# A decoder layer on one core: the first norm's shift and scale by halves, queries and keys in one 512-wide projection, and the MLP operands of the last 512 tokens in two steps

## The chip, the cores and the metric

One core of a Trainium2 chip runs the whole kernel in one launch. The metric is the time of that launch in device microseconds. The engines are TensorE (PE in the profile, its weight loads PEld), VectorE (DVE), ScalarE (ACT), GpSimd (POOL) and SyncE (SP), which issues most of the transfers. Each engine works through its own list of instructions in order; semaphores make one engine wait for another.

## What is computed

The reference is one layer of a decoder: 1024 tokens of width 1024, in float32.

```
h  = rmsnorm(x, g_mix) * (1 + scale_a) + shift_a      # scale, shift, gate: columns of act(c) @ ada_w + ada_b
qkv = h @ w_in                                         # 2960 columns, four groups of 4 heads x 64
o  = [differential, forgetting, stick-breaking, sparse attention] per head group
x1 = x + gate_a * (o @ w_out)
h2 = rmsnorm(x1, g_ffn) * (1 + scale_m) + shift_m
u  = h2 @ w_up ; gate, val = split(u)                  # 2 x 2816 columns
out = x1 + gate_m * ((silu(conv3(gate)) * val) @ w_down)
```

The six vectors (shift, scale and gate for the two sub-layers) are each a product of one vector of 1024 with a 1024 x 1024 block of `ada_w`, 4 MB each.

## The kernel before

The program first writes down all its operations in program order (`K.mm`, `K.act`, `K.dma` and so on), with the tiles that they read and write. Each tile has a class with a quota of buffers. `K.schedule` then plans: it gives every operation a time from a table of costs, and on each engine takes the one that is earliest in program order among those that are ready. What comes out is a fixed list for each engine; on the chip nothing is reordered. Line 393 is the place where every operation is recorded, so all instructions have that line in the profile, and tiles tell them apart.

Every product of two float32 matrices is made from three matmuls: each operand is split into a high part (a cast to the format of fp32r) and a low part (operand minus high part), and high x high, low x high and high x low are added in one PSUM bank.

The start of the program goes like this. `load_x(0)` loads four tiles of 128 tokens (`x`) and scales their rows by the root mean square. `ada_part(1)` and then `ada_part(0)` form the scale and the shift: for each of 8 blocks of 128 rows of `ada_w` (1024 columns, tile `ada`) VectorE does one multiply-add into `acc`, and TensorE then sums the 128 partitions by matmuls against ones (`Xa<-ones,acc`, one column for each of the 8 blocks of 128 features). `norm_x` (line 701) transposes x on TensorE (`X`) and calls `modulate` (line 738): ScalarE applies scale and shift while it moves the bank to `hx`, VectorE casts the high part of `hT`, VectorE or GpSimd subtracts for the low part. The index k counts the 8 blocks of 128 features, and a product with `w_in` adds up all 8.

`proj` (line 765) loads a piece of `w_in`, splits it (the cast on ScalarE, the subtraction on GpSimd) and multiplies it with the tokens, one bank for each tile of 128 tokens (j, 8 of them). Before the change there are four such projections ahead of the attention: queries of group A (`p_aq`, 256 columns), values of group A (`p_va`, 256), values and small columns of C, D and B (`vcd`, 400) and keys of group A (256). Beside them, `ada_rest` forms the other four vectors, in 64 blocks of 512 columns (`ada2`); `merge` mixes its operations into the program, 9.0 planned microseconds apart. Attention follows, group A, C, D and B (`S` are scores, `T` transposes, `O` outputs), with later projections (`pP`) mixed in.

After attention comes the output projection (`op`), and for each half of 512 tokens the second norm: four tiles `xn` are transposed (`oy`), ScalarE applies shift and scale, and the MLP's operands are formed. The MLP uses seven products of quarter blocks in place of eight, so it needs sums and differences of the two token halves: for each of 4 blocks, four subtractions (`hf`, `hk`) and five operands `gB`, each split into a cast and a subtraction. `up` are the banks of the first MLP product, `fr` raw weights, `fw` split ones. Products 1 and 2 (`mul_first`) need the first token half only (`gA`); the five others need `gB`, in the order 6, 5, 7, 3, 4.

Of the kernel before, what the change touches and what calls it, by code (L numbers as in the profile page):

```python
# [69 lines left out]
class AP:  # L70


    def __init__(self, t, steps=(), p=None, shadow=None):
        self.t, self.steps = t, steps
        if shadow is None:
# [36 lines left out]
    def region(self):  # L112
        lo, hi = int(self.shadow.min()), int(self.shadow.max())
        if self.t.space == "PSUM":
            return 0, 128, lo // 512 * 512, hi // 512 * 512 + 511
        return self.p[0], self.p[1], lo, hi
# [28 lines left out]
class Program:  # L145
# [29 lines left out]
    def op(self, alts, reads, writes, kind="c"):  # L175
# [5 lines left out]
        for ap in reads:  # L181
            t = ap.t
            r = ap.region()
            for q, j in t.writes:
                if q[0] < r[1] and r[0] < q[1] and q[2] <= r[3] and r[2] <= q[3]:
# [3 lines left out]
        for ap in writes:  # L189
            t = ap.t  # L190
            r = ap.region()
            for lst in (t.writes, t.reads):
                keep = []
                for q, j in lst:
                    if j != o.i and q[0] < r[1] and r[0] < q[1] and q[2] <= r[3] and r[2] <= q[3]:
                        pred.add(j)
                        if r[0] <= q[0] and q[1] <= r[1] and r[2] <= q[2] and q[3] <= r[3]:
# [314 lines left out]
def layer_kernel(ctx: ExitStack, tc, x, c, rel_bias, ada_w, ada_b, norm_mix_g, norm_ffn_g, w_in, w_out,  # L512
# [32 lines left out]
    for name, quota, group, phase in (  # L545

# [104 lines left out]

    def ada_cols(m, accs, name, pcls):
# [36 lines left out]

    def load_x(half):  # L690
# [10 lines left out]
    def norm_x(half, xns):  # L701
        for k in range(8):
# [4 lines left out]

    x0 = load_x(0)
    acc = ada_part(1)
# [8 lines left out]
    b_ada, g_mix, g_ffn = cols[:, 0:48], cols[:, 48:56], cols[:, 56:64]  # L718
    rows = K.tile("hx", (128, 128))
# [5 lines left out]
    sc_a, = ada_cols(1, [acc], "sc_a", "Xa")  # L725
    a1_a = mod_gain(sc_a, g_mix, "a1_a")
    vt = ps1("Xa")
    K.tr(vt[:, :7], rows[0:7], ident[:7, :7])
    gcols = const([128, 7], name="gcols")
    K.copy(gcols, vt[:, :7], ("DVE",))  # L730

    for a, f in ((1, -math.sqrt(32.0)), (3, -8.0), (5, -8.0), (6, -8.0)):
        K.ts(gcols[:, a:a + 1], gcols[:, a:a + 1], f, None, OP.mult)
    g_aq, g_ak, g_bq, g_bk, g_dq, g_kc, g_sw = (gcols[:, a:a + 1] for a in range(7))
    acc = ada_part(0)
    *_, sh_a = ada_cols(0, [acc[:, halves(n)] for n in range(2)], "sh_a", "Xa")

    def modulate(src, k, half, a1, sh, hi, lo, hcls):
# [4 lines left out]
        K.tt(lo(k, tk), hf, hi(k, tk), OP.subtract, ("DVE", "POOL"))  # L743
# [15 lines left out]
    def split_w(hcls, raw, shape):  # L759
        hi, lo = blk(hcls, F32R, shape), blk(hcls, F32R, shape)  # L760
        K.copy(hi, raw, ("ACT",))
        K.tt(lo, raw, hi, OP.subtract, ("POOL",))
        return hi, lo

    def proj(pieces, n, post, wcls="wh", rcls="wr", kp=2, early=False):

        hi, lo = [], []
        for k0 in range(0, 8, kp):
            raw = K.tile(rcls, (128, kp, n))
            o = 0  # L770
            for c0, m in pieces:
                K.dma(raw[:, :, o:o + m], dap(w_in, k0 * 128 * 2960 + c0, [[2960, 128], [128 * 2960, kp], [1, m]]),
                      512 * kp * m)
                o += m
            h, l = split_w(wcls, raw, (128, kp, n))
            hi += [h[:, t, :] for t in range(kp)]
            lo += [l[:, t, :] for t in range(kp)]
        yield 0

        g = 512 // n  # L780
# [18 lines left out]
    def qk_post(outs, norm=None):  # L799


        def f(jj, ps):
            q = K.tile("nt", (128, 2, 256))
            K.copy(q, ps.split(256))
            if norm:
# [163 lines left out]
    def post_va(j, ps):  # L969
        K.copy(VA.two(j), ps.split(64))  # L970

# [53 lines left out]
    def post_vcd(j, ps):  # L1025
        if j == 0:
            VD.append(K.tile("VD", (128, NT, 2, 64)))
        K.copy(VC[j], ps[:, 0:256].split(64))
        K.copy(VD[0][:, j], ps[:, 256:384].split(64))
# [84 lines left out]
    def attn_D(p, st):  # L1114
        qf, bias, biasC = st
        for i0 in (0, 4):
# [31 lines left out]
            for br in (1, 2):  # L1148
                o = ps1("O")
                l = small("dl", 16)  # L1150
                for i in range(i0, i0 + 4):
# [7 lines left out]
                    pv_pair(P, n, lambda j: [VD[0][:, k0 // 128 + j, br - 1, :]] * 2, o[:, (i - i0) * 128:(i - i0 + 1) * 128])  # L1159
# [605 lines left out]
```

## Time and profile before

| | |
|---|---|
| median of 3 runs | 1467.6 us (1467.43 to 1468.78) |
| profiled execution | 1466.4 us |
| its span, first to last instruction | 1464.5 us |
| mean granted TensorE clock | 0.973 of full speed |
| TensorE busy | 1375.4 us, 94% |
| VectorE busy | 1100.9 us, 75% |
| ScalarE busy | 717.6 us, 49% |
| GpSimd busy | 198.0 us, 14% |
| moved by the DMA engines | 211 MB, 144 GB/s |

The span is that of the profiled execution, and all times of day below count from its first instruction. A row of the view in order of time gives the start, the length from the first to the last of a run of like instructions, and in brackets how long the engine was idle before and what ended that. Matmuls overlap, so a row's length includes the tail of its last one.

### The profile page before, as it was taken

Reading aid. Unit: us, or ns where it says so; the run is one execution under the profiler, and the core shown is the slowest. Engines: PE = TensorE matmul, PEld = TensorE weight load, DVE = VectorE, ACT = ScalarE, POOL = GpSimd, SP = SyncE. Lnnn points to the kernel's source line nnn. Section 1 sums busy time; section 2 is a strip of 40 time slices with the busy share of each in tenths; the row PEclk is TensorE's granted clock in tenths of the full one; section 3 lists DMA queues with packets and bytes.
Section 4 is the critical chain, followed back from the end, with each engine's and each line's share of the span. In section 5 each row is a group of like instructions: output and inputs, shape, how many; then the busy total and the mean of one; then the engine's idle time right before and its main releaser. Section 6 shows DMA issues by size and latency. Waiting matters only on the chain.

```text
span 1464.5 us, 24046 instructions
## 1 busy us (share of the span) xinstructions
PE 1375.4 (94%) x8573; PEld 1169.1 (80%) x8573; DVE 1100.9 (75%) x2301; ACT 717.6 (49%) x1547; POOL 198.0 (14%) x225
## 2 busy tenths in 40 slices
PE   3999999989799999999999699999999999999998
PEld 2879998888589887787788578888888888888887
DVE  7955669988788987577866976666666665898787
ACT  2530256657587765445754644444334344443242
POOL 4633120222223364100000000000000000000000
PEclk6799999999899999999999899999999999999999
DMA  9579463635421445433335132222222225963665
GB/s 358 198 228 304 153 167 107 179 88 145 122 67 52 123 154 160 143 100 92 82 105 190 64 104 87 77 76 78 86 87 87 83 90 202 373 208 100 230 248 171
DMA packets 169961, 211.22 MB, mean 144 GB/s; under 512 B 25517, under 2 KB 112214, under 8 KB 169842
## 3 DMA queue, kind: packets, MB, share of 16 engines
q1 hardware_dynamic: 168338, 208.52, 45.0%
q0 software_dynamic: 1504, 1.17, 0.4%
q8 instruction: 67, 1.10, 0.3%
q14 instruction: 52, 0.43, 0.1%
HBM read 165.30 MB, written 47.89 MB: 146 GB/s over the span
## 4 chain that ended last, share of the span: by engine, by line
PE 61%; DVE 9%; ACT 2%; issue 1%; DMA 1%; POOL 0%; SPq 0%; POOLq 0%; DVEq 0%; ACTq 0%
PE up L393 29%; PE dn L393 13%; PE T L393 5%; PE pP L393 5%; DVE P L393 4%; PE O L393 3%; PE op L393 3%; PE S L393 3%; ACT P L393 1%; DVE m L393 1%; DVE S L393 1%; DVE pt L393 0%; DVE gB L393 0%; DMA dg<-d_g 0%; PE oy L393 0%
## 5 line engine op out<-in xcount | busy, mean ns | idle before, releaser
L393 PE MATMUL up<-gB,fw 128*128 128x512 f32 x1320 | 306.0, 391 | 12.0 <-DVE fw L393 10.3
L393 PEld LDWEIGHTS up<-gB,fw 128*128 128x128 f32 x1320 | 248.7, 189 | 65.5 <-DVE fw L393 10.8
L393 PE MATMUL dn<-ds 128*128 128x512 f32 x924 | 210.3, 389 | 0.5 <-ACT ds L393 0.3
L393 PEld LDWEIGHTS dn<-ds 128*128 128x128 f32 x924 | 173.1, 188 | 37.4 <-DVE ds L393 1.0
L393 PE MATMUL pP<-wh,hT 128*128 128x256 f32 x1344 | 195.9, 289 | 1.3 <-ACT nt L393 0.7
L393 PEld LDWEIGHTS pP<-wh,hT 128*128 128x128 f32 x1344 | 176.0, 191 | 6.8 <-issue 1.9
L393 ACT ACTIVATE P<-S,nm 128x512 f32<-128x512 f32 (+3 forms) x240 | 135.3, 571 | 76.4 <-DVE nm L393 58.5
L393 PE MATMUL S<-kst,qst 128*128 128x512 f32 (+2 forms) x480 | 135.3, 370 | 6.4 <-DVE P L393 3.2
L393 PE MATMUL T<-ident,P 128*128 128x128 f32 x696 | 112.8, 281 | 17.5 <-ACT P L393 11.3
L393 PE MATMUL up<-gA,fw 128*128 128x512 f32 x528 | 124.5, 390 | 0.0
L393 PEld LDWEIGHTS up<-gA,fw 128*128 128x128 f32 x528 | 98.8, 188 | 20.3
L393 PEld LDWEIGHTS T<-ident,P 128*128 128x128 f32 x696 | 80.3, 141 | 37.0 <-ACT P L393 17.2
L393 PEld LDWEIGHTS S<-kst,qst 128*128 128x128 f32 x480 | 78.6, 193 | 17.3 <-DVE P L393 4.9
L393 ACT COPY pt<-T 128x512 f32<-128x512 f32 (+1 forms) x107 | 57.3, 542 | 61.1 <-PE T L393 59.0
L393 DVE TENSOR_REDUCE m<-S 128x1 f32<-128x512 f32 (+3 forms) x160 | 76.8, 490 | 8.9 <-PE S L393 8.5
L393 ACT CAST ds<-dg 128x512 fp32r<-128x512 f32 x82 | 48.1, 619 | 64.3 <-DVE dg L393 42.4
L393 DVE TENSOR_TENSOR fw<-fr,fw 128x512 fp32r<-128x512 f32 x110 | 75.0, 684 | 0.0
L393 DVE COPY pt<-T 128x512 f32<-128x512 f32 (+1 forms) x93 | 57.0, 623 | 21.4 <-PE T L393 19.9
L393 ACT CAST fw<-fr 128x512 fp32r<-128x512 f32 x110 | 67.5, 614 | 9.0 <-DVE fw L393 8.5
L393 ACT ACTIVATE P<-P 128x128 f32<-128x128 f32 (+8 forms) x98 | 64.8, 690 | 13.7 <-POOL P L393 11.2
L393 ACT COPY u<-up 128x512 f32<-128x512 f32 x44 | 25.9, 588 | 87.5 <-PE up L393 87.5
L393 DVE SCALAR_TENSOR_TENSOR cv<-ga,ccol,cv 128x1023 f32<-128x1023 f32 (+1 forms) x44 | 56.5, 1283 | 15.8 <-ACT cv L393 15.0
(286 smaller groups left out, 2341.1 us busy)
## 6 DMA issues: line engine op xcount, KB each, us to landing
dg<-d_g SPq DMA_DIRECT2D x99, 256.0 KB
fr<-in_ffn_w_up_dram SPq DMA_DIRECT2D x88, 256.0 KB
ada<-in_ada_w_dram SPq DMA_DIRECT2D x64, 256.0 KB
dg<-in_ffn_w_down_dram SPq DMA_DIRECT2D x55, 256.0 KB
d_g<-va SPq DMA_DIRECT2D x22, 512.0 KB
ada<-in_ada_w_dram SPq DMA_DIRECT2D x16, 512.0 KB
wr<-in_w_in_dram SPq DMA_DIRECT2D x32, 256.0 KB
x<-in_x_dram SPq DMA_DIRECT2D x8, 512.0 KB
```

Source lines behind the costliest of these rows:

```text
L393: return getattr(getattr(self.nc, eng), meth)(*a, **k)
```

## The change

1. `ada_pair(h)` replaces `ada_part(1)` and `ada_part(0)`: one tile holds 512 columns of the shift and the same 512 of the scale, so that four of the eight blocks k are ready after 8 multiply-adds, and the other four after 8 more. `pair_cols` sums them and forms the two coefficients.
2. Queries and keys of group A are one projection of 512 columns (`p_first`), whose weights are loaded and subtracted in two halves (`cut`), k below 4 ahead of the second half of `ada_w`; the subtraction is on VectorE. Values of group A go into the projection of 400 columns in place of those of C, and the values of C are a projection of 256 columns of their own, the last one.
3. The low part of the normed input is formed on VectorE alone. Transposes of x have 3 banks in place of 6, the sums 1 in place of 2.
4. `ada_rest` is mixed in 6.0 planned microseconds apart in place of 9.0, and the gate that held back loads (`K.hold`) is gone.
5. The second norm of the last 512 tokens and its MLP operands are made in two groups of 256 tokens.
6. The first weights of the MLP (`up_first` of the first two blocks) come earlier in the plan (`K.bias`).

```diff
+    def ada_pair(h):
+        acc = K.tile("acc", (128, 2, 512))
+        for k in range(8):
+            w = K.tile("ada", (128, 2, 512))
+            K.dma(w, dap(ada_w, k * 128 * 6 * D + h * 512, [[6 * D, 128], [D, 2], [1, 512]]), 524288)
...
+    def pair_cols(h, acc):
+        ps, k = ps1("Xa"), slice(4 * h, 4 * h + 4)
+        for u in (1, 0):
+            for c in range(4):
+                K.mm(ps[:, u * 4 + c:u * 4 + c + 1], acc[:, u, c * 128:(c + 1) * 128], ones[:, 0:1], True, True)
+        K.tt(a1_a[:, k], ps[:, 4:8], b_sc[:, k], OP.add)
+        K.tt(a1_a[:, k], a1_a[:, k], g_sc[:, k], OP.mult)
+        K.tt(sh_a[:, k], ps[:, 0:4], b_ada[:, k], OP.add)
...
-        K.tt(lo(k, tk), hf, hi(k, tk), OP.subtract, ("DVE", "POOL"))
+        K.tt(lo(k, tk), hf, hi(k, tk), OP.subtract)
...
-    p_aq = qk_proj("aq", CA_Q, g_aq, 32, True)
-    p_va = proj([(CA_V, 256)], 256, post_va, "vw", "vr", 4, True)
-    next(p_aq)
-    norm_x(0, x0)
-    K.hold = K.ops[-1]
-    next(p_va)
-    K.hold = None
-    steps(p_aq, 4)
+    vd = [(CA_V, 256), (CD_VS, 64), (CD_VW, 64), (CB_F, 4), (CD_G, 12)]
+    p_first = proj([(CA_Q, 512)], 512, post_first, "vw", "vr", 2, True, True)
+    next(p_first)
+    norm_x(0, x0, range(0, 4))
+    acc1 = ada_pair(1)
+    next(p_first)
+    pair_cols(1, acc1)
...
+    norm_x(0, x0, range(4, 8))
+    steps(p_first, 4)
     norm_x(1, load_x(1))
...
-                yield 9.0
+                yield 6.0
...
-    merge(ahead(p_aq, p_va, proj(vcd, 400, post_vcd, "vw", "vr", 2, True), qk_proj("ak", CA_K, g_ak, 32, True), begun=2),
+    merge(ahead(p_first, proj(vd, 400, post_vd, "vw", "vr", 2, True),
+                proj([(CC_V, 256)], 256, post_vc, early=True), begun=1),
...
-    for half in range(2):
-        xns = []
-        for q in range(4):
+    for half, g0, g1 in ((0, 0, 4), (1, 0, 2), (1, 2, 4)):
+        xns, cw = [], slice(g0 * 128, g1 * 128)
+        for q in range(g0, g1):
...
     for f in range(EARLY):
+        K.bias = -300.0
         up_first(f)
+        K.bias = 0.0
         mul_first(f)
```

TensorE's list at the start of the program, before (`Xa` sums, `X` transposes, `S` products, 256 columns wide, with the weights `wh` of the queries and `vw` of the values):

```order
L393 MATMUL Xa<-ones,acc 128x1 x8
L393 MATMUL Xa<-ident,hx 128x7
L393 MATMUL Xa<-ones,acc 128x1 x8
L393 MATMUL X<-ident,x 128x128 x8
L393 MATMUL S<-wh,hT 128x256 x96
L393 MATMUL X<-ident,x 128x128 x6
L393 MATMUL S<-vw,hT 128x256 x5
```

and the same place after:

```order
L400 MATMUL Xa<-ones,acc 128x1 x8
L400 MATMUL X<-ident,x 128x128 x16
L400 MATMUL S<-vw,hT 128x512 x39
L400 MATMUL Xa<-ones,acc 128x1 x8
L400 MATMUL S<-vw,hT 128x512 x3
L400 MATMUL Xa<-ident,hx 128x7
L400 MATMUL S<-vw,hT 128x512 x4
L400 MATMUL X<-ident,x 128x128 x4
L400 MATMUL S<-vw,hT 128x512 x50
```

The second column sums have moved behind 39 products, which need the first four k alone.

TensorE's list ahead of the first scores of attention (`S<-kst,qst`), before (`fl` are the forget logits, `pP` the queries of group C, which attention doesn't need until later):

```order
L393 MATMUL S<-wh,hT 128x256 x9
L393 MATMUL pP<-wh,hT 128x256 x36
L393 MATMUL T<-ident,fl 4x128 x4
L393 MATMUL pP<-wh,hT 128x256
...
L393 MATMUL pP<-wh,hT 128x256 x81
L393 MATMUL S<-kst,qst 128x128
L393 MATMUL pP<-wh,hT 128x256 x5
```

and after:

```order
L400 MATMUL S<-wh,hT 128x256 x55
L400 MATMUL T<-ident,fl 4x128 x3
L400 MATMUL T<-acc_1765,ones 1x512
L400 MATMUL T<-ident,fl 4x128
L400 MATMUL S<-kst,qst 128x128
L400 MATMUL T<-ident,fl 4x128 x4
L400 MATMUL S<-kst,qst 128x128 x3
L400 MATMUL pP<-wh,hT 128x256 x50
```

The products `pP` have moved behind the first scores, and the last sums of `ada_rest` (`acc_1765`) stand right ahead of them.

VectorE's list around the operands of the second token half, before (the last of four `xn`, then the operands):

```order
L393 TENSOR_SCALAR xn<-x_10474,rms_y 128x1024
L393 TENSOR_TENSOR fw<-fr,fw 128x512
L393 TENSOR_TENSOR ga<-up,p_10596 128x512
L393 TENSOR_TENSOR fw<-fr,fw 128x512
L393 TENSOR_TENSOR hf<-hf,hk 128x512
L393 CAST gB<-hf 128x512
L393 TENSOR_TENSOR hf<-hf 128x512
```

and after (the second of four `xn`, then the first group's operands; `x_10260` is the output projection of the next tile of tokens, `oT` its input for the one behind):

```order
L400 TENSOR_SCALAR xn<-x_10121,rms_y 128x1024
L400 TENSOR_TENSOR hf<-hf,hk 128x256
L400 CAST gB<-hf 128x256 x2
...
L400 TENSOR_TENSOR hf<-hf,hk 128x256
L400 TENSOR_TENSOR x_10260<-op,x_10260 128x512
L400 TENSOR_TENSOR fw<-fr,fw 128x512 x2
...
L400 TENSOR_TENSOR x_10260<-op,x_10260 128x512
L400 TENSOR_TENSOR oT<-ox,oT 128x512
```

Operands of 256 columns now stand between the sums of the output projection, and `oT` of the last tile behind them.

## Rows read from the trace of the kernel before

**Rows 1.** Page: busy time by engine; TensorE's clock in 40 slices.

```profile
PE 1375.4 (94%) x8573; PEld 1169.1 (80%) x8573; DVE 1100.9 (75%) x2301; ACT 717.6 (49%) x1547; POOL 198.0 (14%) x225
PEclk6799999999899999999999899999999999999999
```

**Rows 2.** Busy time by stage; columns are in the first line.

```profile
core 0: us, PE busy (x) PEld busy (x) DVE busy (x) ACT busy (x) POOL busy (x), PEclk, DMA share, GB/s
0.00:40.50 40.50, 15.06 (x67) 13.09 (x68) 30.08 (x57) 13.02 (x27) 17.92 (x31) 0.68 0.97 364
...
75.80:112.70 36.90, 34.39 (x228) 27.80 (x228) 20.71 (x41) 14.88 (x30) 12.52 (x10) 0.95 0.81 236
112.70:156.30 43.60, 41.13 (x218) 40.72 (x218) 25.63 (x53) 2.95 (x9) 9.95 (x17) 0.92 0.94 311
...
200.20:319.80 119.60, 110.77 (x938) 98.73 (x937) 108.43 (x365) 76.67 (x233) 24.59 (x21) 0.99 0.50 140
792.70:843.60 50.90, 38.86 (x176) 30.57 (x174) 45.09 (x87) 32.35 (x61) 0.00 (x0) 0.87 0.28 94
```

**Rows 3.** TensorE in order of time: start, length, operation, [idle before <- releaser].

```profile
23.34 3.57 PE L393 MATMUL Xa<-ones,acc 128*128 128x1 f32 x16 [6.34 <-DVE acc L393]
...
35.53 3.54 PE L393 MATMUL Xa<-ones,acc 128*128 128x1 f32 x16 [8.42 <-DVE acc L393]
...
40.54 3.33 PE L393 MATMUL S<-wh,hT 128*128 128x256 f32 x14
45.98 12.62 PE L393 MATMUL S<-wh,hT 128*128 128x256 f32 x82 [2.11 <-POOL hT L393]
```

**Rows 4.** VectorE and GpSimd in order of time.

```profile
15.32 7.96 DVE L393 SCALAR_TENSOR_TENSOR acc<-ada,cact,acc 128x1024 f32<-128x1024 f32 x6
...
33.04 5.93 POOL L393 TENSOR_TENSOR wh<-wr,wh 128x512 fp32r<-128x512 f32 x4 [19.30 <-DMA wr<-in_w_in_dram]
33.05 2.34 DVE L393 SCALAR_TENSOR_TENSOR acc<-ada,cact,acc 128x1024 f32<-128x1024 f32 x1
...
39.97 0.75 DVE L393 CAST hT<-hx 128x512 fp32r<-128x512 f32 x2
...
799.93 0.16 DVE L393 SCALAR_TENSOR_TENSOR rms_t<-rms_ss,rms_t 128x1 f32<-128x1 f32 x1
```

**Rows 5.** TensorE in order of time: long rows at the full clock.

```profile
112.71 14.86 PE L393 MATMUL S<-vw,hT 128*128 128x400 f32 x80
...
190.25 9.96 PE L393 MATMUL pP<-wh,hT 128*128 128x256 f32 x81
...
873.48 13.76 PE L393 MATMUL up<-gB,fw 128*128 128x512 f32 x60
```

**Rows 6.** TensorE's gaps ahead of attention, and one stretch of 2 us.

```profile
50.00:52.00 2.00, 2.00 (x12) 2.00 (x12) 1.97 (x2) 0.13 (x2) 2.00 (x2) 0.56 1.04 382
...
84.41 1.01 PE L393 MATMUL T<-nt,tab 33*8 33x512 f32 x2 [2.51 <-DMA nt<-in_onehot_dram]
...
130.04 1.64 PE L393 MATMUL T<-ones,acc 128*128 128x1 f32 x8 [2.47 <-DVE fg L393]
```

**Rows 7.** TensorE in order of time: attention's first score; where the lists meet.

```profile
200.05 0.22 PE L393 MATMUL S<-kst,qst 128*128 128x128 f32 x1
...
319.76 1.70 PE L393 MATMUL S<-kst,qst 128*128 128x512 f32 x4
```

**Rows 8.** TensorE in order of time, start of the MLP.

```profile
838.09 1.65 PE L393 MATMUL up<-gB,fw 128*128 128x512 f32 x3 [10.33 <-DVE fw L393]
...
843.62 24.59 PE L393 MATMUL up<-gB,fw 128*128 128x512 f32 x106 [0.68 <-ACT u L393]
```

**Rows 9.** VectorE: two rows in order of time; a group of 256 columns.

```profile
833.74 1.89 DVE L393 TENSOR_TENSOR gB<-hf,gB 128x512 fp32r<-128x512 f32 x3
835.55 0.69 DVE L393 TENSOR_TENSOR gB<-hk,gB 128x512 fp32r<-128x512 f32 x1
...
L393 DVE SCALAR_TENSOR_TENSOR hl<-T,hl 128x256 fp32r<-128x256 f32 x16 | 6.3, 419 | 0.9 <-ACT hl L393 0.5 <-issue 0.2
```

More of the change, by code (lines that the diff above doesn't have):

```diff
@@ L114, in region, with columns @@
         if self.t.space == "PSUM":
-            return 0, 128, lo // 512 * 512, hi // 512 * 512 + 511
-        return self.p[0], self.p[1], lo, hi
+            return 0, 128, lo // 512 * 512, hi // 512 * 512 + 511, *self.lane
+        return self.p[0], self.p[1], lo, hi, *self.lane
+    def columns(self, a, b):
+        v = self[(slice(None),) * len(self.shadow.shape) + (slice(a, b),)]
+        v.lane = a, b
+        return v
     def build(self):
@@ L650, in ada_part @@
         return acc
+    def ada_pair(h):
[3 more added lines that the diff above has]
+            K.dma(w, dap(ada_w, k * 128 * 6 * D + h * 512, [[6 * D, 128], [D, 2], [1, 512]]), 524288)
+            if k == 0:
+                K.ts(acc, w, cact[:, k:k + 1], None, OP.mult)
+            else:
+                K.stt(acc, w, cact[:, k:k + 1], acc, OP.mult, OP.add)
+        return acc
     def ada_cols(m, accs, name, pcls):
@@ L699, in load_x, with norm_x @@
         return xns
-    def norm_x(half, xns):
-        for k in range(8):
+    def norm_x(half, xns, ks=range(8)):
+        for k in ks:
             ps = ps1("X")
@@ L723, in layer_kernel @@
     K.dma(rows[6:7], nsa_knorm_g[0, 1:3].rearrange("(o r) p -> o (r p)", o=1), 512, "POOL")
[L725 to L736, printed above, removed]
+    pair_cols(0, acc0)
     def modulate(src, k, half, a1, sh, hi, lo, hcls):
@@ L771, in proj @@
             for c0, m in pieces:
-                K.dma(raw[:, :, o:o + m], dap(w_in, k0 * 128 * 2960 + c0, [[2960, 128], [128 * 2960, kp], [1, m]]),
+                K.dma(raw.columns(o, o + m), dap(w_in, k0 * 128 * 2960 + c0, [[2960, 128], [128 * 2960, kp], [1, m]]),
                       512 * kp * m)
                 o += m
-            h, l = split_w(wcls, raw, (128, kp, n))
+            h, l = split_w(wcls, raw, (128, kp, n), "DVE" if cut else "POOL")
             hi += [h[:, t, :] for t in range(kp)]
             lo += [l[:, t, :] for t in range(kp)]
+            if cut and k0 + kp == 4:
+                yield 0
         yield 0
-        g = 512 // n
+        g = min(2, 512 // n)
         for j in range(NT):
@@ L804, in f, with one, rest @@
             K.copy(q, ps.split(256))
+            rest(jj, q)
+        def one(j, ps):
+            if j % 2 == 0:
+                pend.append(K.tile("nt", (128, 2, 256)))
+            K.copy(pend[-1][:, j % 2, :], ps)
+            if j % 2:
+                rest(j // 2, pend[-1])
+        pend = []
+        f.one = one
+        def rest(jj, q):
             if norm:
@@ L1023, in layer_kernel, with post_vc, post_vd @@
     gates = const([128, NT, 12], name="gates")
-    def post_vcd(j, ps):
+    def post_vc(jj, ps):
+        K.copy(VC.two(jj), ps.split(64))
+    def post_vd(j, ps):
         if j == 0:
-            VD.append(K.tile("VD", (128, NT, 2, 64)))
-        K.copy(VC[j], ps[:, 0:256].split(64))
-        K.copy(VD[0][:, j], ps[:, 256:384].split(64))
+            VD.append(K.tile("VD", (128, NT, 128)))
+        K.copy(VA[j], ps[:, 0:256].split(64))
+        K.copy(VD[0][:, j], ps[:, 256:384])
         K.copy(fg[:, j], ps[:, 384:400], ("DVE",))
@@ L1488, in layer_kernel @@
         for k in (0, 4, 1, 5, 2, 6, 3, 7):
-            ps = ps1("oy")
-            for q in range(4):
-                K.tr(ps[:, q * 128:(q + 1) * 128], xns[q][:, k * 128:(k + 1) * 128], ident)
-            v = kept[half, k] = hb("hf" if half else "hk")
+            ps = ps1("oy")[:, :cw.stop - cw.start]
+            for q, xn in enumerate(xns):
+                K.tr(ps[:, q * 128:(q + 1) * 128], xn[:, k * 128:(k + 1) * 128], ident)
+            v = kept[half, k] = hb("hf" if half else "hk")[:, :ps.n]
             K.act(v, ps, AF.Identity, bias=sh_m[:, k:k + 1], scale=a1_m[:, k:k + 1])
```

68 lines of the change are left out of this document (42 added, 26 removed), and 6 rows, old and new, of the table k.

## The prediction, made before the changed kernel was timed

> **What bounds the kernel now.** I read the page's slices first, then the busy time by stage, then TensorE's instructions in order of time at the two stages that the change touches. The page says that TensorE is the engine to watch: 94% busy, and at the full clock in nearly every slice [rows 1]. The two slices that are not are the first one and the one around 840 us, which are the two places of the change. By stage [rows 2], TensorE worked 15.1 of the first 40.5 us, while VectorE worked 30.1 and the DMA engines were 97% busy. What TensorE waits for there stands in [rows 3]: the column sums of the scale (23.34 us) and of the shift (35.53) each stand behind VectorE's accumulators, and the first projection matmul starts only at 40.54. It starts at the low clock: 14 matmuls of 256 columns took 3.33 us, 0.24 each, twice the 0.123 below; from 50 to 52 us 0.56 was still granted [rows 6], so the rise is near 51.7. VectorE's accumulator goes at 1.33 us for 1024 columns [rows 4], about as fast as the weights land, so the 16 of them are the length of this stage; one next to a GpSimd subtraction took 2.34.
>
> The second place: TensorE runs dry at 827.8 us, waits 10.33 us, then runs at half clock until 843.6 [rows 8], with VectorE busy without a pause on the operands gB.
>
> **The prices.** Matmuls at the full clock, all in long rows [rows 5]: 13.76/60 = 0.229 us for 512 columns, 14.86/80 = 0.186 for 400, 9.96/81 = 0.123 for 256.
>
> **Part 1, the start.** TensorE's first product needed all 16 accumulator steps; now it needs 8, since half of the scale and half of the shift arrive together. The first eight end as before at 23.3 us (six in 7.96 from 15.32 [rows 4]). From the start of the last column sums to the first product before took 40.54 - 35.53 = 5.0 us [rows 3]; the new order puts two accumulator steps (0.65 and 1.3) in between, so the first product starts at about 23.5 + 5.0 + 1.9 = **30.5 us**, 10 earlier. The two weight subtractions that now go to VectorE (1024 columns, about 1.2 each, twice 0.605 of [rows 9]) stand beside the column sums (3.57 us at the low clock), so they cost nothing; on GpSimd they took 5.93 for four of half that size [rows 4] and slowed VectorE.
>
> From 30.5 us TensorE has 48 products (four token tiles, k below 4). A product of 512 costs 0.44 at the low clock (0.238 x 0.229/0.123). Before, the clock rose 5.7 us after the work resumed at 45.98; I take 6.5 us here: 15 products until 37, 33 at 0.229 until 44.6, with 1.8 for the second column sums inside. VectorE meanwhile: four splits of the normed input (a cast of 0.375 [rows 4] and a subtraction of 0.6 each) to 33.7, six accumulators to 41.7, so the other four k arrive from 46.4 on, just as TensorE runs out. 48 more products end at **58 us**. At 58.4 before, 96 products of 256 were done; now 96 of 512 are. The wider ones also save 384 x 0.123 - 192 x 0.229 = 3.2 us over the whole projection, counted in the sums below. [...]
>
> **Part 2, the second 512 tokens (58 to 78).** VectorE does here what GpSimd shared before (all 8 low parts of the normed input), beside the norms of q and k and the accumulators of later coefficients. Its list from about 50 us to the last scaled x tile is six accumulator steps of 512 columns (0.67, half of 1.33), four scalings of x (0.75, two casts), six operations on q and k (some 0.45) and 18 on one column (0.16 [rows 4]): 12.6, to 62.5. Then eight splits (7.8) with some 4 us of q and k between them: 74.5. GpSimd subtracts weights at the same time, which slows VectorE [rows 4], so I take 78. TensorE has by then 38 of 96 products; 58 are left. The bounds are 75 and 82. Part of the head start goes here: TensorE idles.
>
> **Part 3, to the first score of attention.** Before, this was 75.8 to 200.05 [rows 7] = 124.3 us. The products in it are 507 of 256 columns and 192 of 400: 62.4 + 35.7 = 98.1. Lost are two gaps of 2.51 and 2.47 [rows 6], with mean clocks of 0.95 over 36.9 us and 0.92 over 43.6 [rows 2], 1.8 and 3.5: 10.3 in all. The other 15.9 is small work (lookups, row sums, transposes), which stays. After, from 78: 58 x 0.229 + 192 x 0.186 + 198 x 0.123 = 13.3 + 35.7 + 24.4 = 73.4, with 15.9: 167.3. For gaps, between 0 and 10.3, I take 4, since the accumulators of later coefficients are issued earlier (6.0 for 9.0): **171.3**. Transfers: from 78 some 26 MB must land (53 blocks of 262 KB, 15 writes of q and k, the skewed tables, 24 loads of k); at the 311 GB/s of 112.7 to 156.3 [rows 2] that is 84 us, to 162, so the queues just keep up.
>
> **Part 4, attention.** In the two orders TensorE's list is the same again from the scores at 319.76 [rows 7] until the last output projection. Before, 118 products of the next projection (pP) were done ahead of the first score, now 6. The other 112 x 0.123 = 13.8 us must fit beside attention. From 200.2 to 319.8 TensorE was busy 110.8 of 119.6 and VectorE 108.4 [rows 2]: hidden in full they cost 0, not at all 13.8. TensorE's 8.8 idle us hold about half; I take 6. So 171.3 + 119.7 + 6 = 297.0 in place of 319.76: **22.8 us gained**. From there the order is the same, so it is carried to the end.
>
> **Part 5, MLP operands in two steps.** VectorE's work is 36 operations of 512 columns, (835.55 - 833.74)/3 = 0.605 apart; they become 72 of 256, for which [rows 9] has 0.419 own time where the 512 has 0.69, so some 0.34 apart: 24.5 for 21.8, 2.7 us more. What is gained is part of VectorE's idle time there, 5.8 of 50.9 us [rows 2], and that three to six products of the first stalled group are left when the last operand comes, not ten: 1 to 1.6 us. The last output projection now waits for its oT, which on VectorE stands behind half of the first group's operands; 12 products of the next stage, whose weights are loaded earlier by the bias, fill that. Last operand at about 843 in place of 842: I take **1 us gained**, between 3 lost (the clock low again where it resumes) and 4 gained. [...]
>
> Nothing else costs: smaller bank quotas (X 6 to 3), more slots for raw weights, and copies of 256 columns on ScalarE, which worked 77 of 120 us in attention.
>
> **Sum.** The profiled execution took 1466.4 us: 1466.4 - 22.8 - 1 = 1442.6. The median of the runs is 1.2 above the profiled one: 1443.8, say **1444 us**.
>
> **Rivals.** (a) The queues become the bound: SyncE issues in order, and between 75.8 and 112.7 moved only 236 GB/s [rows 2]. At that rate the 26 MB take 110 us, the first score comes at 190, and the gain is 22.8 - 18.7 + 1 = 5: 1463. For it: 0.94 busy until 156; against: what held it were loads behind finished tiles, not bandwidth. Chance 0.11. (b) Attention hides all 112 products and no gap is left: 10 more, 1434 or below; chance 0.05 below. (c) Nothing comes of it: the start is given back in part 2 and attention costs all 13.8: 22.8 - 7.8 - 4 - 6 - 3 = 2, 1465; chance 0.05. (d) Slower: TensorE's clock stays at the low level because its rows are broken by waits on VectorE. Gaps of 2.5 us were followed by the low clock [rows 6]. Each 512 product then costs 0.21 more. It decides from about 120 of the 192 beyond the 15 counted (25 us); all of them, less 7 us that only fill idle time, make 177 x 0.21 - 7 = 30: 1474. Against: rows of 39 and 50 products stand without a break in the order. Chance 0.07.
>
> **The numbers.** The forecast with its own spread (1435 to 1456): 0.72. The range, 1432 to 1460, takes in (b) and the nearer half of (a) and leaves out (c), (d) and the rest, some 0.18. A measurement here tells 0.2% (3 us) from no change: faster 0.72 + 0.11 + 0.05 = 0.88, same 0.05, slower 0.07.
>
> **What would show it.** First product at 30 to 32 us; 96 products of 512 by 59; the first score near 171, and the scores of 319.76 near 297; the wait of 10.33 split into shorter ones and dense MLP work from about 820. Wrong would be: a low clock after 40 us, a first score after 185, or dense MLP work later than 835.

## The result, and the profile after

The changed kernel took 1453.8 us (median of 4 runs, 1452.5 to 1454.4) where the kernel before took 1467.5 beside it: a ratio of 0.9908, with a 95% interval of 0.9890 to 0.9927. Faster was right, and 1453.8 lies in the range of 1432 to 1460. But the forecast was 1444: of some 24 us that were expected, 13.7 came. The profiled execution took 1454.4 us, with a span of 1452.7. Two executions that took far longer than the others of their kernel (5269.6 us of c_after, 1719.3 us of e8_lookups_pool) are left out of all times below.

The page of the kernel after: busy time by engine, and TensorE's granted clock in 40 slices, which answer to [rows 1].

```profile
PE 1371.6 (94%) x8381; PEld 1152.3 (79%) x8381; DVE 1102.4 (76%) x2352; ACT 722.1 (50%) x1581; POOL 177.0 (12%) x211
PEclk9999999999899999999999999999999999999999
```

TensorE is still 94% busy. The first slices are recorded at the full clock now and the one near 840 us too. So what was gained must show as fewer TensorE microseconds or fewer idle ones, and both can be summed. The busy time of the kernel after, by stage, up to the scores at which the two lists meet; the last line is the sum:

```profile
core 0: us, PE busy (x) PEld busy (x) DVE busy (x) ACT busy (x) POOL busy (x), PEclk, DMA share, GB/s
0.00:57.00 57.00, 36.59 (x164) 29.71 (x165) 46.11 (x95) 27.65 (x59) 14.17 (x29) 1.00 0.97 330
57.00:78.00 21.00, 17.09 (x88) 13.50 (x87) 20.05 (x48) 11.12 (x22) 14.18 (x10) 0.92 0.50 142
78.00:177.64 99.64, 89.00 (x520) 76.36 (x518) 63.03 (x123) 25.31 (x62) 24.23 (x29) 0.98 0.87 273
177.64:309.81 132.17, 124.89 (x1054) 113.41 (x1054) 114.96 (x373) 81.73 (x241) 19.77 (x16) 0.99 0.43 118
sum 309.81, PE 267.57 PEld 232.97 DVE 244.14 ACT 145.81 POOL 72.36; mean PE 66.89 PEld 58.24 DVE 61.03 ACT 36.45 POOL 18.09
```

The same sum for the kernel before, up to the same scores at 319.76:

```profile
sum 319.76, PE 275.68 PEld 251.14 DVE 244.05 ACT 145.62 POOL 95.44; mean PE 91.89 PEld 83.71 DVE 81.35 ACT 48.54 POOL 31.81
```

The mark moved by 9.95 us. TensorE was busy 275.68 - 267.57 = 8.1 us less, and idle 44.1 - 42.2 = 1.9 us less. The start alone lost 5 us of idle time (25.4 of 40.5 us in [rows 2], 20.4 of 31.5 after). At the mark 1.9 of it is left; the rest came back as idle time further on. So most of what was gained is busy time. Up to the mark there are 192 matmuls fewer (1826 in place of 2018), as many as the wide projection saves; by the long rows they are worth 3.2 us. The other 4.9 us are about what the rows of the start give: the second column sums took 1.92 us in place of 3.54, and the first 96 products took some 0.8 us more than the long rows' price of 0.229 (39 in 9.76 us, below) in place of 4.1 more (14 in 3.33 us and 82 in 12.62, [rows 3], where one takes 0.123).

TensorE at the start, in order of time (start, length, operation, [idle before <- releaser]):

```profile
23.73 3.57 PE L400 MATMUL Xa<-ones,acc 128*128 128x1 f32 x16 [6.92 <-DVE acc L400]
27.16 1.95 PE L400 MATMUL X<-ident,x 128*128 128x128 f32 x8
...
31.52 9.76 PE L400 MATMUL S<-vw,hT 128*128 128x512 f32 x39
41.32 1.92 PE L400 MATMUL Xa<-ones,acc 128*128 128x1 f32 x16
...
45.51 11.62 PE L400 MATMUL S<-vw,hT 128*128 128x512 f32 x50
```

This stage went as foreseen: the first product at 31.52 (before 40.54), then 96 products of 512 columns by 57.1 us with hardly a break. The 39 products took 9.76 us, 0.250 each. Estimated from that, only about four of them ran at half rate, where 15 were expected: (9.76 - 39 x 0.229)/0.21 = 4; the first took 0.776 us from its start to its end, those around 34 us 0.39. The estimated number belongs in part to this execution (see the two kernels again, below).

Then TensorE's longest gap ahead of attention, the first score, and the scores where the lists meet:

```profile
107.83 0.32 PE L400 MATMUL T<-ident,nt 128*128 128x128 f32 x1 [4.99 <-DVE nt L400]
...
177.64 0.30 PE L400 MATMUL S<-kst,qst 128*128 128x128 f32 x1
...
309.81 0.97 PE L400 MATMUL S<-kst,qst 128*128 128x512 f32 x4
```

What TensorE waited for from 57 to 178 us (what waited, for what: us in total, times, longest):

```profile
PE T L400 <- DVE nt L400: 5.0, 1, 5.0
PE T L400 <- DVE acc L400: 2.9, 3, 1.4
PE X L400 <- DVE x L400: 2.4, 2, 1.3
PE T L400 <- DMA nt<-in_onehot_dram: 1.8, 1, 1.8
```

The first score came 22.4 us earlier than in [rows 7], the meeting scores only 9.95. Of the two waits of [rows 6], 1.8 and 0.8 us are left; the longest ones of this stage are new or longer than before. And one thing lost its margin: VectorE's last steps for the later vectors, before and after (VectorE alone, in order of time):

```profile
161.40 2.30 DVE L393 SCALAR_TENSOR_TENSOR acc<-ada,cact,acc 128x512 f32<-128x512 f32 x3
```

```profile
168.98 7.54 DVE L400 SCALAR_TENSOR_TENSOR acc<-ada,cact,acc 128x512 f32<-128x512 f32 x6
```

Before, the last of the 64 steps ended at 163.7, 36 us ahead of the first score. Now it ends at 176.5, 12.8 us later and 1.1 us ahead of the first score, although the steps were planned closer together.

The start of the MLP, TensorE and then VectorE:

```profile
823.08 0.50 PE L400 MATMUL up<-gB,fw 128*128 128x512 f32 x1 [1.40 <-ACT gB L400]
...
834.47 22.77 PE L400 MATMUL up<-gB,fw 128*128 128x512 f32 x97
...
862.51 13.76 PE L400 MATMUL up<-gB,fw 128*128 128x512 f32 x60
```

```profile
833.16 1.10 DVE L400 TENSOR_TENSOR gB<-hf,gB 128x256 fp32r<-128x256 f32 x3
834.17 0.43 DVE L400 TENSOR_TENSOR gB<-hk,gB 128x256 fp32r<-128x256 f32 x1
```

The wait of 10.33 us of [rows 8] is gone. In its place stand waits of 1.4 us and less, and dense work begins as the last operand is there, at 834.5. Three operations of 256 columns follow each other in (1.10 - 0.43)/2 = 0.335 us, as costed. The row of 60 products, 873.48 in [rows 5], starts at 862.51: 10.97 earlier, 1.0 more than the meeting scores. Behind it the span gains another 0.8 (590.2 in place of 591.0).

### The profile page after: what moved, and what is told of

Its sections match the earlier page's. It is cut to its first block, busy times and chain, and to the rows that moved or that the text cites. A ratio compares the mean times of both kernels' runs of the same rounds, so it can differ in the third digit from the quotient of the medians.

```text
span 1452.7 us, 23740 instructions
## 1 busy us (share of the span) xinstructions
PE 1371.6 (94%) x8381; PEld 1152.3 (79%) x8381; DVE 1102.4 (76%) x2352; ACT 722.1 (50%) x1581; POOL 177.0 (12%) x211
## 4 chain that ended last, share of the span: by engine, by line
PE 51%; DVE 3%; DMA 1%; ACT 0%; issue 0%; SPq 0%; DVEq 0%; ACTq 0%
PE up L400 28%; PE dn L400 14%; PE op L400 3%; PE T L400 2%; PE O L400 2%; PE S L400 1%; DVE gB L400 1%; DVE m L400 0%; DVE hf L400 0%; DMA oin<-o_dram 0%; PE pP L400 0%; PE oy L400 0%; DVE pu L400 0%; ACT P L400 0%; DVE S L400 0%
## 5 line engine op out<-in xcount | busy, mean ns | idle before, releaser
L400 PE MATMUL S<-kst,qst 128*128 128x512 f32 (+2 forms) x480 | 132.0, 367 | 6.1 <-DVE P L400 3.2
L400 PE MATMUL S<-vw,hT 128*128 128x512 f32 (+1 forms) x384 | 87.8, 381 | 0.3 <-DVE hT L400 0.3
L400 PEld LDWEIGHTS S<-vw,hT 128*128 128x128 f32 x384 | 71.3, 193 | 11.0 <-issue 3.2
L400 DVE SCALAR_TENSOR_TENSOR acc<-ada,cact,acc 128x512 f32<-128x512 f32 (+1 forms) x70 | 64.4, 920 | 11.3 <-DMA ada<-in_ada_w_dram 10.2
L400 ACT ACTIVATE P<-P 128x128 f32<-128x128 f32 (+8 forms) x98 | 64.8, 690 | 15.3 <-POOL P L400 11.8
```

What stands on the lines that cost most here:

```text
L400: return getattr(getattr(self.nc, eng), meth)(*a, **k)
```

## The experiments

Two causes were to be told apart. The first: why 14.6 us of TensorE's time are idle between 57 us and the first score (3.9 up to 78, 10.6 behind it). The second: why attention gave nothing for free. Each kernel's time stands beside runs of the kernel before on the same chip (1466.9 to 1468.4 us).

| run | what is different from the changed kernel | us | ratio to before | first score |
|---|---|---|---|---|
| changed | | 1453.8 | 0.991 (0.989 to 0.993) | 177.6 |
| c_after | nothing | 1454.7 | 0.992 (0.989 to 0.995) | |
| e1_mlp_undone | MLP operands in one step, no bias | 1454.8 | 0.991 (0.989 to 0.993) | 177.3 |
| e3_halves_undone | 16 accumulator steps ahead of the first product | 1457.7 | 0.992 (0.990 to 0.995) | 183.1 |
| e4_lean_cq | 64 products fewer beside attention | 1449.2 | 0.987 (0.985 to 0.989) | 176.7 |
| e2_spacing9 | later vectors 9.0 apart | 1451.9 | 0.990 (0.988 to 0.993) | 177.6 |
| e5b_lookups_after_x | table lookups in the first 20 us | 1451.9 | 0.990 (0.989 to 0.992) | 183.5 |
| e8_lookups_pool | the same, rows written from GpSimd's queue | 1455.4 | 0.992 (0.990 to 0.995) | 190.0 |
| e9_no_qk_norm | no norm of group A's q and k | 1462.3 | 0.996 (0.994 to 0.998) | 179.0 |
| e6_acc_one | later vectors: loads, hardly any steps | 1461.5 | 0.996 (0.995 to 0.998) | 196.5 |
| e10_one_load | later vectors: steps, one load of eight | 1454.7 | 0.990 (0.987 to 0.993) | 173.0 |
| e6c_no_rest | later vectors: neither | 1447.0 | 0.986 (0.984 to 0.988) | 162.3 |

Single runs of one kernel lie up to 9 us apart here (e2_spacing9, 1448.4 to 1457.4), so two rows that differ by 2 or 3 us are not told apart by the times.

### The two kernels again

> The changed kernel again, beside the three variants that follow, as their measure: 1453.8 us, 0.991 of before, with the first product at 31.5 us, the first attention score at 177.6 and the scores where the two lists meet at 309.8. If the granted clock of the first 60 us differs from the first trace (1.00 there, 0.50 from 14.5 to 51.8 us in the kernel before), the clock at the start belongs to the execution and not to the change.

The ratio came out the same, 0.9916 (0.9886 to 0.9945), from runs of 1451.3 to 1457.8 us. The marks of the changed kernel are read from its first trace alone.

> The kernel before once more, for a second trace of its start: the profiled executions differ in the granted clock that they record (0.973 to 0.985 in the mean for this kernel). Either the first products run at 0.24 us for 256 columns until about 51.7 us again (the low clock belongs to the order of this start), or at 0.123 from 41 or 42 us on (it belongs to the execution, and some 5 us of the gap between the two first traces are chance).

The kernel before, again: 1466.7 us. TensorE at its start, and then the stretch in which the first 14 products stand:

```profile
41.37 3.25 PE L393 MATMUL S<-wh,hT 128*128 128x256 f32 x14
46.80 11.57 PE L393 MATMUL S<-wh,hT 128*128 128x256 f32 x82 [2.19 <-POOL hT L393]
```

```profile
41.00:46.00 5.00, 3.62 (x18) 3.41 (x16) 4.97 (x12) 4.65 (x8) 2.84 (x1) 1.00 1.00 371
```

The 14 products ran at 0.232 us each again, at half speed, and the 82 behind them took 1.5 us more than 82 x 0.123. That this start runs its first products at half rate (0.24 and 0.232 us in place of 0.123) thus doesn't belong to one execution. How long that lasts does in part: the 82 products took 1.0 us less than in [rows 3]. The changed kernel's start varies too. Six of the kernels below have the same row of 39 products behind the same first column sums; it took 9.90 to 11.13 us there, the longest in e10_one_load:

```profile
31.44 11.13 PE L400 MATMUL S<-vw,hT 128*128 128x512 f32 x39
```

By the same reckoning that is five to ten products at half rate, and the four of the first trace are the fewest of seven. Whether the gap of 2.2 us between the products is what kept the rate low in the kernel before was not tested.

### The MLP operands in one step again

```diff
-    for half, g0, g1 in ((0, 0, 4), (1, 0, 2), (1, 2, 4)):
+    for half in range(2):
...
-        K.bias = -300.0
         up_first(f)
-        K.bias = 0.0
```

> The changed kernel with the MLP operands of the last 512 tokens made in one step again, and without the bias on the first MLP weights. Theory of the prediction: this part was worth 1 us, so 1455. By the two traces (10.97 us ahead at the first product of the second block against 9.3 at the last long row of the output projection) it was worth 1.7 there and perhaps 0.8 behind it: 1455.5 to 1456.5. [...]

It took 1454.8, 1.0 more than the changed kernel. TensorE in its trace:

```profile
308.67 0.98 PE L400 MATMUL S<-kst,qst 128*128 128x512 f32 x4
...
827.97 1.65 PE L400 MATMUL up<-gB,fw 128*128 128x512 f32 x3 [10.33 <-DVE fw L400]
...
863.36 13.76 PE L400 MATMUL up<-gB,fw 128*128 128x512 f32 x60
```

The wait of 10.33 us is back, to the hundredth. From the meeting scores to the row of 60 it takes 554.7 us, and 552.7 with the operands in two steps. By the traces the part is worth 1 to 2 us; by the times it is not told from nothing.

### The halves undone

```diff
-    pair_cols(0, acc0)
+    acc1 = ada_pair(1)
+    pair_cols(0, acc0)
...
-    norm_x(0, x0, range(0, 4))
-    acc1 = ada_pair(1)
     next(p_first)
     pair_cols(1, acc1)
...
-    norm_x(0, x0, range(4, 8))
+    norm_x(0, x0)
```

> The changed kernel with one thing undone: all 16 accumulator steps and both column sums stand ahead of the first product again; queries and keys stay 512 wide, and all else stays. Theory A, the start counts in full: first product near 41 us, all later marks 9 to 10 us later, 1463. Theory B, the head start is mostly handed back between 57 and 178 us, where TensorE idles 14.6 us behind norms, table lookups and accumulators that have their own pace: first product near 41, first score only 3 to 5 later than 177.6, 1457 to 1459.

1457.7 us, 3.9 more than the changed kernel. TensorE's first product, the row of 60, and the stretch from 57 us to the first score:

```profile
39.88 1.20 PE L400 MATMUL S<-vw,hT 128*128 128x512 f32 x2
...
866.29 13.76 PE L400 MATMUL up<-gB,fw 128*128 128x512 f32 x60
```

```profile
57.00:183.06 126.06, 116.64 (x639) 98.29 (x638) 84.98 (x168) 36.91 (x88) 35.54 (x36) 0.95 0.78 240
```

The first product comes 8.4 us later, the first score 5.4 (a little more than theory B's 3 to 5), the row of 60 3.8. Theory B holds by the marks: more than half of the head start is given back, step by step. The idle time shows how. Up to 57 us TensorE idles 25.2 us, 4.8 more than in the changed kernel, and from there to the first score 9.4, 5.1 less; the sum is the same, and the 5.4 us are busy time. By the times, 1453.1 to 1458.6 here and 1451.3 to 1457.8 for c_after on the same chip, the difference isn't clear of the noise. If the halves are worth some 4 of the 13.7 us, the MLP's part 1 to 2 and the rest, 8 or so, the wide projection and what was changed with it, that rest is a difference: no run undoes the wide projection, or the gate that is gone, alone.

### What a product costs beside attention

```diff
-                for a, b in ((hT_hi, hi), (hT_lo, hi), (hT_hi, lo)):
+                for a, b in ((hT_hi, hi), (hT_lo, hi), (hT_hi, lo))[:2 if lean else 3]:
...
-("cq", qk_proj("cq", CC_Q, 0.125))
+("cq", qk_proj("cq", CC_Q, 0.125, lean=True))
```

> The changed kernel with 64 of the 192 products of group C's queries left out (high x low is not added, so these queries are less exact); they stand beside attention of group A, between the first score and the meeting scores. It prices one product there. Theory A, attention hides none, since TensorE's list is as full as the plan can make it: 64 x 0.123 = 7.9 us less, 1446. Theory B, as the prediction put it, half of them lie in TensorE's idle time: 4 us less, 1450.

1449.2 us, 4.6 less than the changed kernel by the medians, and 1446.1 in the profiled execution, 8.3 less. TensorE just ahead of its first score, the first score and the meeting scores:

```profile
169.96 6.88 PE L400 MATMUL pP<-wh,hT 128*128 128x256 f32 x56
176.68 0.22 PE L400 MATMUL S<-kst,qst 128*128 128x128 f32 x1
...
299.97 0.98 PE L400 MATMUL S<-kst,qst 128*128 128x512 f32 x4
```

Between the marks it takes 123.3 us in place of 132.2, 8.9 less. But here too the lists were dealt anew: 64 products pP stand ahead of the first score, where the changed kernel has 6. So 120 are missing between the marks (450 in place of 570) and not 64, which makes 0.074 us each where a product takes 0.123, and the clock differs as well (0.97 and 0.99). The run doesn't price a product beside attention, and by the times it lies between the two theories. It shows something else: the 58 products more ahead of the first score didn't make it later. From 57 us to the first score TensorE idles 8.2 us here and 14.6 in the changed kernel.

What prices the products is the stage itself, before and after, since the attention work between the first and the meeting scores is the same in both. With 1054 matmuls there in place of 938, TensorE was busy 14.1 us longer than in [rows 2], its idle time went from 8.8 to 7.3 us only, and the stage took 12.5 us longer. The kernels e1 and e2, which keep this list, took 131.4 and 129.9 us for it, 11.7 and 10.2 longer than before. So attention hides little of the 14: 1.5 to 4 us.

### Later vectors farther apart

```diff
-                yield 6.0
+                yield 9.0
```

> The changed kernel with the operations of the four later vectors mixed in 9.0 planned microseconds apart again, not 6.0. If accumulators in VectorE's list ahead of the norms of q and k hold TensorE up (theory A), the waits of 5.0 us at 107.8 and of 3.8 us in all for sums shrink and the first score comes at 172 to 174, 1450. If the buffers of the norms are what it waits for (theory B), the 5.0 us stay, and the last sums come later: first score 178 or later, 1454 to 1456.

```profile
107.93 0.45 PE L400 MATMUL T<-ident,nt 128*128 128x128 f32 x1 [4.85 <-DVE nt L400]
...
177.63 0.31 PE L400 MATMUL S<-kst,qst 128*128 128x128 f32 x1
...
307.56 1.70 PE L400 MATMUL S<-kst,qst 128*128 128x512 f32 x4
```

The wait stays, 4.85 us, and so does the first score. The spacing in the plan has no part in it: the last of the 64 steps ends at 176.5 us, as in the changed kernel. The time, 1451.9, is not told from that of the changed kernel.

### The table lookups early

```diff
+    for n0 in range(0, NOH, 1024):
+        oh = blk("x")
+        K.dma(oh[:33, :n], onehot[:, n0:n0 + n], 33 * 4 * n)
...
+        K.dma(frow[:, n0:n0 + n], oh[:8, :n], 32 * n)
     acc0 = ada_pair(0)
```

> The changed kernel with the five table lookups of the relative bias (T from tab and the onehot rows) moved into the first 20 us, where TensorE idles, with buffers of their own (those of x, not nt). In the first trace of the changed kernel the wait of 5.0 us at 107.8 ends with a norm that waited for an nt buffer, which a lookup's row held until its write had landed; another 1.8 us is waited for the onehot rows. Theory B: first product 1 to 1.4 later (0.3 MB more ahead of it), 4.8 us of lookups, the 1.8 and 4 of the 5.0 gone, first score near 168, 1445 to 1447. Theory A, accumulators on VectorE set the pace there: only the lookups' own 4.8 less 1.4 come through, 1450 to 1451.

1451.9, not 1446. The gap behind the onehot rows is gone, but not the others. The two long gaps of TensorE between 57 us and the first score:

```profile
67.26 1.28 PE L400 MATMUL T<-ident,nt 128*128 128x128 f32 x4 [5.46 <-DVE nt L400]
...
113.30 0.45 PE L400 MATMUL T<-ident,nt 128*128 128x128 f32 x1 [5.00 <-DVE nt L400]
```

No lookup holds an nt buffer there any more, and a wait of 5 us is there all the same. In the changed kernel the norm ahead of 107.8 did wait for such a row: ScalarE idled 2.1 us at 102.4 until a write of `frow` had landed. Taking that away brought another wait in its place, so theory B's gain did not come. (The first score came 5.8 us later here, and yet the MLP's row of 24 products, 857.08 in the changed kernel, 2.8 earlier: behind the first score this list stands in another order, so that mark can't be compared across the two.) What VectorE and GpSimd did just before:

```profile
107.36 1.86 DVE L400 SCALAR_TENSOR_TENSOR qk_t<-qk_y 128x16 f32<-128x16 f32 x1
109.15 2.42 DVE L400 SCALAR_TENSOR_TENSOR acc<-ada,cact,acc 128x512 f32<-128x512 f32 x1
```

```profile
103.10 7.91 POOL L400 TENSOR_TENSOR vw<-vr,vw 128x800 fp32r<-128x800 f32 x4 [3.59 <-DMA ada<-in_ada_w_dram]
```

The norm's operation of 16 columns took 1.86 us (0.16 in the median of its kind), and the accumulator step behind it, which stands in the list between two steps of the norm, 2.42 (0.74 for the one at 112.08, with no subtraction of GpSimd beside it), beside four subtractions of GpSimd of about 2 us each. In [rows 4], too, a step of 1024 columns took 2.34 us beside such a subtraction, and 1.33 without. Why the two take longer side by side was not shown.

```diff
-        K.dma(frow[:, n0:n0 + n], oh[:8, :n], 32 * n)
+        K.dma(frow[:, n0:n0 + n], oh[:8, :n], 32 * n, "POOL")
```

> The kernel with the early lookups (e5b), with their rows written from GpSimd's queue in place of SyncE's. In e5b the rows kept buffers of x until 64 us, so that the last tiles of x came late and TensorE waited 5.5 us at 67 and 4.4 us for x. If that is the cause, both waits shrink to below 2 us each, and the scores that stood at 304.00 there come near 299; 1446 to 1448. If VectorE is late there for another reason, both stay: 1452.

It got worse: 1455.2 to 1459.7 us, with the first score at 190.0. Between 57 us and there TensorE waited 8.8 us for x (4.4 in e5b) and 8.1 us for ScalarE's hx. So writing the rows from the other queue doesn't bring x earlier: its last two loads are issued at 57.3 and 59.0 here and from 58.6 on in e5b. Whether the rows' buffers are what holds them stays open, and so does what held hx.

### The norm of q and k left out

```diff
-    post_aq, post_ak = (qk_post([split_out((name, p), s) for p in range(2)], (32, 0)).one
+    post_aq, post_ak = (qk_post([split_out((name, p), s) for p in range(2)], None).one
```

> The changed kernel without the norm of group A's queries and keys (copies and transposes stay; the result is wrong): the chain from a bank of q and k to its transposes loses a square, a sum, a root and a product. Theory D: the wait of 5.0 us at 107.8, the 0.9 and 0.3 near 60 and the low clock behind the former (1 us) go, first score at 170 to 172, 1447. Theory A: VectorE's accumulators and the sums are the pace, first score at 175 or later, 1451 to 1453.

Neither: 1462.3 us, 8.5 slower with less to do. The first score comes at 179.0 and the meeting scores at 314.5.

The wait of 5.0 us is gone, but the plan dealt all lists anew, and others came: 2.7 us for x at 63, 4.1 for hT at 70, 4.5 for an accumulator at 123. Attention took 135.4 us, at a clock of 0.96 (0.99 in the changed kernel). The run doesn't decide between the theories. It shows that leaving work out can cost more than the work did, once the lists are dealt anew.

### The later vectors left out, in parts

```diff
             K.dma(w, ada_w[0, k * 128:(k + 1) * 128, c0:c0 + n], 512 * n)
+            if k:
+                continue
```

> The changed kernel with 56 of the 64 accumulator steps of the four later vectors left out (their weights are still loaded, the vectors are wrong): some 41 us less work on VectorE between 57 and 178 us. Theory A, accumulators on VectorE are what TensorE's idle 14.6 us there come from: first score at 168 to 170, 1445. Theory B, buffers of the norms and the lookups: only the waits for sums (3.8 us) go, the 5.0 us at 107.8 stay, first score at 173 to 175, 1450.

1461.5 us, slower again. SyncE's issues and TensorE's second half of the first products:

```profile
34.27 9.52 SPq L400 DMA_DIRECT2D ada<-in_ada_w_dram  x8
...
44.83 6.44 SPq L400 DMA_DIRECT2D ada<-in_ada_w_dram  x11
```

```profile
53.62 20.18 PE L400 MATMUL S<-vw,hT 128*128 128x512 f32 x84
```

With no steps to wait for, the buffers of the later vectors come free at once, and 19 loads of 256 KB stand in SyncE's list ahead of the weights of the next projections (6 in the changed kernel). TensorE's list is another one as well: 12 products stand ahead of the second sums, and the other 84 of 96 behind transposes that waited 2.4 and 2.2 us for x, so that they began at 53.6. The run mixes these things, so it doesn't decide either. It does show that VectorE's steps are also what keeps these loads back. The next two kernels leave out loads and steps, and then only the loads:

```diff
-        for k in range(8):
+        for k in range(1):
```

> The changed kernel with 56 of the 64 blocks of the four later vectors left out altogether, loads and accumulator steps (the vectors are wrong): 14.7 MB less to move and some 41 us less on VectorE, nearly all of it before 178 us. It bounds from above what these vectors cost ahead of attention. Theory A, VectorE and the queues set TensorE's idle time there (14.6 us between 57 and 178): the first score comes at 165 to 168, 1442 to 1445. Theory D, the chain of the norm of q and k (copy, square, sum, root, product, transpose) is simply longer than the products that TensorE's list puts beside it: only the waits for sums (3.8 us) and half of the wait of 5.0 go, first score 171 to 174, 1448 to 1450.

1447.0 us, and 1444.4 in the profiled execution. TensorE from 57 us to the first score, and 24 products ahead of the row of 60 (857.08 in the changed kernel):

```profile
57.00:162.30 105.30, 103.15 (x608) 87.91 (x608) 42.12 (x120) 35.10 (x80) 30.33 (x35) 1.00 0.56 159
```

```profile
847.12 5.60 PE L400 MATMUL up<-gA,fw 128*128 128x512 f32 x24
```

Theory A holds: without the later vectors TensorE idles 2.2 us of this stage and not 14.6, the clock stays at full speed, and the first score comes 15.3 us earlier. The chain of the norm is short enough when VectorE and the queues are free for it. At the row of 24, 10.0 of the 15.3 are left, at the end by the times 6.9, less than the 9 to 12 that were expected.

```diff
+            if k == 0:
                 w = K.tile(wcls, (128, n))
                 K.dma(w, ada_w[0, k * 128:(k + 1) * 128, c0:c0 + n], 512 * n)
```

> The changed kernel with all 64 accumulator steps of the four later vectors but only one of eight loads (each step reads the first block again; the vectors are wrong): 14.7 MB less to move, VectorE's work as in the changed kernel. Without loads and steps (the run e6c_no_rest) the first score came at 162.3 and not at 177.6; this one tells which of the two did it. Theory Q, the loads and their queue: first score at 162 to 167, about 1447. Theory V, VectorE's steps ahead of other work in its list: first score at 173 to 178, 1452.

1454.7 us. The same two rows:

```profile
57.00:173.02 116.02, 109.50 (x616) 91.78 (x615) 82.73 (x172) 38.38 (x95) 38.14 (x39) 0.96 0.52 145
```

```profile
857.06 5.60 PE L400 MATMUL up<-gA,fw 128*128 128x512 f32 x24
```

With the steps and hardly any loads the first score lies at 173.0, at the end of theory V's range: 4.6 of the 15.3 us come from the loads, 10.7 only when VectorE's steps go too. By idle time the shares are others: 6.5 us idle here, so 8.0 of 12.4 went with the loads; the clock was lower in this execution (0.96 of the stage). Both take part, and their shares are not settled. At the row of 24 nothing of the 4.6 is left.

None of these kernels that compute the whole layer beats the changed one by more than the runs can tell: e2 and e5b, at 1451.9, have intervals that hold its ratio.

## Why the prediction was right, and where it was 10 us off

**The start: right.** First product at 30.5 forecast, 31.52 measured; 96 products by 58 forecast, 57.1 measured. The half rate cost less than expected (an estimated 4 products, not 15), which paid for the later start; other kernels with this start lost five to ten products to it, so that is in part luck. The price of a wide product, 0.229 us, stands in the long rows after as before: 13.76/60. The saving of 3.2 us over the projection follows from it, but it was not measured alone.

**Second 512 tokens: right.** Of the 96 products of this half, 58 were to be left at 78 us; counted in the trace, 42 were done then and 54 left.

**To the first score: the gaps were mis-sized.** From 78 us on, 89.3 us of work were forecast, and TensorE was busy 89.0. The step that failed is "For gaps, between 0 and 10.3, I take 4, since the accumulators of later coefficients are issued earlier". It was 10.6, a little beyond the upper bound, and that is the whole 6.3 us between 171.3 and 177.64. The reason given was wrong as well: with the old spacing the first score came at the same 177.6. What the prediction did not see is that the later vectors, 16.8 MB and 64 steps, fill the shorter stage to its end: before, they were done 36 us ahead of the first score, now 1.1 us. Without them (e6c) the idle time is nearly nil; how much of it is due to the loads and how much to the steps is not settled. The prediction had counted the transfers, at 311 GB/s; 273 were moved here. Rival (a) was no bound of the stage, but a part of it is in these gaps.

**Attention: the wrong half.** The other step that failed is "TensorE's 8.8 idle us hold about half; I take 6" for 13.8 us of products moved behind the first score. They cost most of their price: the stage took 12.5 us more than before (10.2 and 11.7 in the other two traces of this list), and its idle time fell by 1.5. The bound was there, "not at all 13.8". The idle time before was in a dozen pieces, all but one of 0.8 us or less; the longest stands just before the meeting scores:

```profile
317.32 1.38 PE L393 MATMUL O<-pt,V 128*64 128x128 f32 x16 [2.66 <-DVE pt L393]
```

In all but two of them the next operation in TensorE's list waits for a step of attention on another engine, whatever else is ready. An average of idle time says nothing about that.

**MLP: right.** 1 us forecast, 1.0 in the two traces, 1 to 2 by the part undone. Dense work did begin with the last operand, at 834.5; "from about 820" was the old mark less 22.8 us, of which 9.95 came, and the sign of being wrong, 835, was missed by half a microsecond. In the trace one operation of 256 columns took 0.43 us and the next began after 0.335, where the prediction had 0.419 and some 0.34.

**The sum.** By the profiled executions: forecast 23.8, measured 12.0. The two mis-sized terms make 6.3 + 6.5 = 12.8, and the MLP and the stretch behind it gave 0.9 back. Of the rivals, (c) named both failures (the start given back, all 13.8 paid), but coupled them with a loss in the MLP and a larger loss in the second 512 tokens. (d) did not come: in the first trace an estimated four products of 512 ran at half rate. Behind 57 to 63 us, of which TensorE was busy 2.6, the granted clock did fall once more, to 0.60 from 63 to 66 us and 0.83 from 66 to 69; the mean between 57 and 78 us was 0.92.

## What to carry to other kernels

Where one engine is over 90% busy (TensorE 94% here), an earlier start is worth only the idle time, and the time at a low rate, that it removes from that engine up to a mark where both lists agree. Sum busy and idle time to that mark, and ask of each other engine whether it can do its unchanged work in the shorter stage. Work of the bound engine that is moved behind a mark costs nearly its full price (10.2 to 12.5 us for 13.8 here), unless the trace shows idle pieces there that the moved work can reach; ahead of the first score, where TensorE idled, 58 more products of the same work didn't make it later in e4. And where a planner deals the lists, leaving a part out also deals them anew: e9, with less to do, was 8.5 us slower, and e4 moved 58 products across the mark that was to price them. So count the work between two marks before comparing the times between them.

## What the runs showed of the hardware

The granted clock of a stretch doesn't always tell the speed. In the changed kernel 1.00 was recorded for all of the first 57 us, and yet 16 column sums took 3.57 us at 23.7 and 1.92 at 41.3, and 8 transposes 1.95 at 27.2, where 6 took 0.82 at 57.0. In the second trace of the kernel before, too, 1.00 stands for the stretch in which products took twice their time (0.232 us for 0.123). At the start of these kernels the rate of the rows tells more.

In the trace of e5b an operation of VectorE of 16 columns took 1.86 us in place of 0.16 beside GpSimd's subtractions of 800 columns. The norm has three operations of this kind, 0.16 to 0.17 us each in the median of that trace, and this one operation is longer than the three together.
